# Down's chunks in pairs with seven-product K pairs in a two-layer hybrid decoder trunk

## The chip, the core and the metric

The kernel runs on one core of one Trainium2 chip. The metric is the device time of one execution in microseconds (us). Before the change the median of three runs was 2584.53 us (2582.99 to 2587.38). One execution was profiled; the trace has every instruction of the engines: PE is TensorE (PEld its weight loads), DVE is VectorE, ACT is ScalarE, POOL is GpSimd, and SP is the queue that issues most DMAs.

## The reference

The input is one sequence of 256 tokens with 2048 features in float32. Two layers follow each other: a Mamba-2 state-space mixer and differential attention, each followed by a SwiGLU feed-forward network (FFN). Each of the four sub-layers has an RMSNorm in front and another behind, and the result is added to the residual stream. What matters here is the FFN, which occurs twice:

```
def swiglu(h, w_gate, w_up, w_down):
    return (jax.nn.silu(h @ w_gate) * (h @ w_up)) @ w_down

h = rmsnorm(x, norm_ffn_pre[i])
x = x + rmsnorm(swiglu(h, ffn_w_gate[i], ffn_w_up[i], ffn_w_down[i]), norm_ffn_post[i])
```

Gate and Up are 2048 by 5632 matrices, Down is 5632 by 2048, all in float32.

## The kernel before

**Products.** The 256 tokens make two token tiles of 128 (t = 0, 1). A weight block is read from memory into a `raw` tile (three buffers) and split into a high part `hi` and a remainder `lo` (four buffers each): ScalarE casts `hi` (line 119), VectorE subtracts to get `lo` (line 120). The token side is split in the same way. A float32 product is then three matmuls: high by high, high by low and low by high. Weights are 512 columns wide, so each matmul moves 512 columns past a 128 by 128 token block.

**The plain form, `mv` (line 158).** One chunk of 512 output columns, with K in steps of 128; each step gives both token tiles a product, into one PSUM tile each. A raw tile holds four K steps of one chunk: 24 matmuls.

**The pair form, `pair` (line 201).** Two chunks of 512 columns go together, K in pairs of steps. A raw tile holds two K steps of two chunks, also 24 matmuls. For the K pairs named in `SEVEN` (2, 4 and 6 of eight) the eight products (two token tiles, two K steps, two chunks) are replaced by seven, as in Strassen's and Winograd's scheme for 2 by 2 blocks: 21 matmuls. For that,
- a DMA on POOL's queue adds one weight quarter to another on its way into memory (line 228),
- VectorE makes three sums of weight quarters (lines 242 to 244), and weights and sums are both split: 1536 columns first, then 2048,
- four sums of token blocks, the token *forms*, are split too and used as the token side,
- after the last seven, VectorE combines four PSUM products (lines 259 to 262) into four corrections, which are added or subtracted when an accumulator is evacuated (`done`).

**The FFN.** Chunk 10 is done alone with `mv`; while its Up runs, `make_form` (line 719 on) makes the three token forms and they stay in three of four `xr` buffers. The eleven chunks of 512 hidden features come in three parts: (10, 0, 1), (2, 3, 4, 5) and (6, 7, 8, 9). In each part every two chunks go through a Gate pair and an Up pair; Gate's result stays in a `t512` tile until TensorE transposes the product of Gate and Up (`act_piece`, line 269 on) into the token side for Down. `t512` has eight buffers used in rotation, and a Gate pair with its Up pair takes all eight. Then `out_proj` (line 596 on) runs Down over the part's K steps, for each of its four chunks of 512 output columns with `mv`, and adds up the parts in the eight `m` tiles. In the third part each output chunk is followed by its row sums of squares on ScalarE and by a product with a row of scales on POOL; the row is read by SP into a single `wpost` buffer. Behind the fourth comes the normalisation chain. The residual `x` is kept in memory during the FFN and read back into `xr` buffers for the third part.

**The order of the work.** A planner places the instructions of each engine by its own costs, earlier lines of the program first where they are ready; on the chip each engine then goes through its list in that order. `later(k, ...)` puts a piece of work k ticks later in the program: `pair` and `mv` tick twice for each raw tile. SP issues the raw loads, scale rows and residual; POOL issues the accumulating loads. Each waits at the head of its list until the buffer is free.

Of the kernel before, what the change touches and what calls it, by code (L numbers as in the profile page):

```python
# [10 lines left out]
F32 = mybir.dt.float32  # L11
# [5 lines left out]
P = 128  # L17
S = 256
NT = 2
# [11 lines left out]
LAG2 = 2  # L31

SEVEN = (2, 4, 6)


@with_exitstack
def trunk_kernel(ctx, tc, x_rows, x_cols, vec_cols, vec64, post_rows, lam_rows,
# [110 lines left out]
    def lookup(dct, key):  # L148
        while key not in dct:
            deferred.popleft()[1]()  # L150
        return dct[key]
# [46 lines left out]
                    evac(ct, acc[ct][:, :S], acc[ct][:, S:])  # L198
            tick()

    def pair(blocks, seven, form, done):

        flush()
        acc = {}  # L210
        end = len(blocks) - 1

        def mm(k, st, hi, lo, last):
            first = k not in acc
            if first:
                acc[k] = (auxp.tile([P, 512], F32, tag="aux", name="cp") if isinstance(k, str) else
                          accp.tile([P, 512], F32, tag="acc", name="acc"))
            for q, (a, b) in enumerate(((st[0], hi), (st[0], lo), (st[1], hi))):
                nc.tensor.matmul(acc[k], a, b, start=first and q == 0, stop=last and q == 2)  # L219

        ss = {}
        for kp, src in enumerate(blocks):
            raw = rawp.tile([P, 4, 512], F32, tag="raw", name="raw")
            for c in range(2):
                nc.sync.dma_start(raw[:, 2 * c:2 * c + 2], src[c])
            if kp in seven:

                nc.gpsimd.dma_start(raw[:, 0:1], src[0][:, 1:2], accum_op=ALU.add)
            if kp not in seven:
                hi, lo = prep(raw)  # L230
                for t in range(NT):
                    for c, e in ((0, 2), (1, 0)):
                        for j in range(2):
                            mm((t, c), x_stat(2 * kp + j, t), hi[:, e + j], lo[:, e + j], kp == end and j == 1)
# [7 lines left out]
            nc.vector.tensor_tensor(raw[:, 2], raw[:, 2], raw[:, 0], op=ALU.add)  # L242
            nc.vector.tensor_tensor(raw[:, 3], raw[:, 3], raw[:, 2], op=ALU.add)
            nc.vector.tensor_tensor(raw[:, 1], raw[:, 2], raw[:, 1], op=ALU.subtract)  # L244
            sh, sl = prep(raw)
            k0, k1 = 2 * kp, 2 * kp + 1
            mm("p1", x_stat(k0, 0), hi[:, 1], lo[:, 1], last)
            mm((0, 0), x_stat(k1, 0), hi[:, 2], lo[:, 2], False)
# [5 lines left out]
            mm((1, 0), x_stat(k1, 1), sh[:, 3], sl[:, 3], False)  # L254
            tick()
            if last:
                s1, u, w, x = (t512(n) for n in ("s1", "su", "sw", "sx"))
                nc.scalar.copy(s1, acc["p1"])
                nc.vector.tensor_tensor(u, acc["p6"], s1, op=ALU.subtract)
# [333 lines left out]
        if not final:  # L593
            later(2, stats)

    def out_proj(w, first, last, acts, kgs, step, final, lag, t512, pw, scale=None, ns=range(4)):

        def sums(t, n):
            mt = m[(t, n)]
            row_sumsq(ss4[t][:, n:n + 1], mt, t512("junk"))  # L600
            dst = t512("mw") if n == 3 else mt
            (nc.vector if n == 3 else nc.gpsimd).tensor_tensor(dst, mt, pw(n), op=ALU.mult)
            return dst

        ss4 = {}
        for n in ns:
            def evac(t, ps, n=n):
                if first:
                    m[(t, n)] = mpool.tile([P, 512], F32, tag="m", name="m")
                    nc.scalar.copy(m[(t, n)], ps)  # L610
                else:
                    nc.vector.tensor_tensor(m[(t, n)], m[(t, n)], ps, op=ALU.add)
                if not last:
                    return
                if t not in ss4:
                    ss4[t] = small.tile([P, 4], F32, tag="ss4", name="ss_m", bufs=3)
                    for e in range(n):
                        sums(t, e)
                dst = sums(t, n)
# [7 lines left out]
            def stat(i, j, t):  # L627
                hi, lo = lookup(acts, (t, kgs[i] // 2))
                jj = (kgs[i] % 2) * 2 + j
                return hi[:, jj], lo[:, jj]  # L630
# [52 lines left out]
    def xr_tile(name, shape=(P, 2, 512), dtype=F32):  # L683
        return postp.tile(list(shape), dtype, tag="xr", name=name, bufs=4)

    def fetch_x(src):
# [15 lines left out]
    xr_d = [[dramp.tile([P, 1024], F32, name=f"xr_d{t}{h}") for h in range(2)] for t in range(NT)]  # L702

    def ffn(wg, wu, wd, step, final):
        acts, gt, forms = {}, {}, {}

        def rs(t):
            return lookup(rstd, (step - 1, t))
# [10 lines left out]
        def make_form(kp):  # L719

            n, k = kp // 2, kp % 2 * 2
            xf = t512("xf", (P, NT, 2, P))
            f = t512("f", (P, 4, P))
            for t in range(NT):
                sl = slice(t * P, (t + 1) * P)
                nc.vector.tensor_tensor(xf[:, t], xT_hi[n][:, k:k + 2, sl].bitcast(F32),
                                        xT_lo[n][:, k:k + 2, sl].bitcast(F32), op=ALU.add)
            nc.vector.tensor_tensor(f[:, 0], xf[:, 1, 0], xf[:, 1, 1], op=ALU.subtract)
            nc.vector.tensor_tensor(f[:, 1], xf[:, 1, 0], xf[:, 0, 0], op=ALU.subtract)
            nc.vector.tensor_tensor(f[:, 2], xf[:, 0, 0], f[:, 0], op=ALU.subtract)  # L730
            nc.vector.tensor_tensor(f[:, 3], xf[:, 0, 1], f[:, 2], op=ALU.subtract)
            ff = forms[kp] = xr_tile("ff", (P, 4, 2, P), F32R)
            split(ff[:, :, 0], ff[:, :, 1], f)

        def form(kp, f):
            ff = lookup(forms, kp)
            return ff[:, f, 0], ff[:, f, 1]

        def g_done(p):
            def done(t, c, ps, ss):  # L740
# [25 lines left out]
            for h in range(2):  # L766
                nc.sync.dma_start(xr_d[t][h].rearrange("p (e k) -> p e k", e=2), xr_of[(t, h)])
        for k, kp in enumerate(SEVEN):
            later(1 + 3 * k, lambda kp=kp: make_form(kp))
        mv([wu[10, k] for k in range(4)], u_stat, u_evac, LAG2)  # L770
        parts = [(10, 0, 1), (2, 3, 4, 5), (6, 7, 8, 9)]
        for pi, part in enumerate(parts):
            for c in part:
                if c < 10 and c % 2 == 0:
                    pair(twos(wg, c), SEVEN, form, g_done(c // 2))
                    pair(twos(wu, c), SEVEN, form, u_done(c // 2))
            last = pi == len(parts) - 1
            if last:
                fetch_x(lambda t, h: xr_d[t][h].rearrange("p (e k) -> p e k", e=2))
            out_proj(wd, pi == 0, last, acts, [2 * c + e for c in part for e in range(2)], step, final, LAG2, t512,  # L780
                     load_post(step) if last else None)

    ffn(w_g0, w_u0, w_d0, 1, False)

# [183 lines left out]
```

## Time and profile before

| what | value |
|---|---|
| median of three runs | 2584.53 us |
| the profiled execution | 2586.13 us |
| its span, first to last instruction | 2584.3 us |
| instructions | 31682, of them 12210 matmuls |
| TensorE busy | 2549.0 us (99%) |
| VectorE busy | 1851.3 us (72%) |
| ScalarE busy | 1300.4 us (50%) |
| mean granted TensorE clock | 0.995 |

Matmuls are pipelined: each is recorded with its whole duration, and neighbours overlap, so their spacing (a stretch's length by the matmuls in it) tells more than their length. A row in order of time gives the start, the length, the engine, the line, the operation, the tile written from the tiles read, the shape, and the number of such rows merged; in brackets stands the idle time in front of it and what ended it.

### The profile page before, as it was taken

The numbers are of one execution on the slowest core, as the hardware profiler recorded it, in microseconds if no ns is written. First come the engines' busy times: TensorE is split into PE (matmuls) and PEld (weight loads), VectorE is DVE, ScalarE is ACT, GpSimd is POOL, SyncE is SP. The second block draws the span as 40 slices with busy tenths as digits, with TensorE's granted clock in tenths as the row PEclk, the third lists the DMA queues.
The fourth block names the chain that finished last, engine by engine and source line by source line (L and its number), as shares of the span: only waits on it lengthen the run. The fifth ranks groups of instructions, "written<-read, shape, count | busy, mean of one in ns | idle before, by whom it ended". The sixth has DMA issues, their size and how long they took to land.

```text
span 2584.3 us, 31682 instructions
## 1 busy us (share of the span) xinstructions
PE 2549.0 (99%) x12210; PEld 2096.6 (81%) x12210; DVE 1851.3 (72%) x2280; ACT 1300.4 (50%) x1524; POOL 213.2 (8%) x224
## 2 busy tenths in 40 slices
PE   8999999999999999999999999999999999999998
PEld 7878888888878888888888788887788888888886
DVE  7888757887677668856885665566578478757874
ACT  4555655555565444534453654445555455435542
POOL 2021000111100000000001100000100000000001
PEclk9999999999999999999999999999999999999999
DMA  6545554544766666756676544444566566656663
GB/s 224 186 140 196 182 199 173 196 165 164 266 216 196 218 203 198 228 212 197 196 251 220 190 147 163 179 147 147 211 200 214 202 207 216 232 182 210 211 248 131
DMA packets 120343, 507.87 MB, mean 197 GB/s; under 512 B 11840, under 2 KB 28544, under 8 KB 84352
## 3 DMA queue, kind: packets, MB, share of 16 engines
q1 hardware_dynamic: 110896, 489.27, 53.7%
q0 software_dynamic: 8640, 15.73, 3.7%
q8 instruction: 96, 1.57, 0.3%
q10 hardware_dynamic: 656, 0.85, 0.1%
q14 instruction: 55, 0.45, 0.1%
HBM read 499.44 MB, written 6.36 MB: 196 GB/s over the span
## 4 chain that ended last, share of the span: by engine, by line
PE 94%; DVE 3%; issue 1%; ACT 1%; POOL 0%; DMA 0%; DVEq 0%; POOLq 0%; ACTq 0%
PE acc L168 40%; PE acc L219 26%; PE acc L193 11%; PE cp L219 6%; PE acc L195 6%; PE sc L844 1%; PE pt_f L273 1%; PE py L500 1%; DVE v L425 1%; DVE lo L120 0%; ACT hi L119 0%; PE ptx L576 0%; PE pyt L510 0%; PE po L879 0%; PE pyo L533 0%
## 5 line engine op out<-in xcount | busy, mean ns | idle before, releaser
L120 DVE TENSOR_TENSOR lo<-raw,hi 128x2048 fp32r<-128x2048 f32 (+2 forms) x548 | 1060.7, 1952 | 558.3 <-ACT hi L119 556.8
L119 ACT CAST hi<-raw 128x2048 fp32r<-128x2048 f32 (+2 forms) x548 | 876.8, 1612 | 882.3 <-DVE raw L244 226.3
L219 PE MATMUL acc<-hi,xT 128*128 128x512 f32 x1840 | 589.1, 390 | 0.0
L193 PE MATMUL acc<-xT,hi 128*128 128x512 f32 x1280 | 458.0, 401 | 0.0
L219 PEld LDWEIGHTS acc<-hi,xT 128*128 128x128 f32 x1840 | 345.2, 188 | 71.3
L195 PE MATMUL acc<-xT,lo 128*128 128x256 f32 x1280 | 360.5, 283 | 5.8 <-DVE lo L120 5.8
L219 PE MATMUL acc<-lo,xT 128*128 128x512 f32 x920 | 358.0, 389 | 0.0
L168 PE MATMUL acc<-hi,xT 128*128 128x512 f32 x1024 | 336.3, 400 | 2.3 <-ACT xT L581 1.9
L193 PEld LDWEIGHTS acc<-xT,hi 128*128 128x128 f32 x1280 | 242.0, 189 | 57.7 <-issue 0.9
L168 PE MATMUL acc<-hi,ah_f 128*128 128x512 f32 x704 | 274.5, 391 | 0.0
L168 PE MATMUL acc<-lo,ah_f 128*128 128x512 f32 x704 | 274.4, 390 | 0.0
L168 PE MATMUL acc<-hi,al_f 128*128 128x512 f32 x704 | 274.3, 390 | 0.0
L195 PEld LDWEIGHTS acc<-xT,lo 128*128 128x128 f32 x1280 | 243.5, 190 | 8.2 <-DVE lo L120 6.4
L168 PEld LDWEIGHTS acc<-hi,xT 128*128 128x128 f32 x1024 | 192.8, 189 | 48.6 <-issue 5.1
L168 PE MATMUL acc<-lo,xT 128*128 128x512 f32 x512 | 207.7, 406 | 1.6 <-DVE lo L120 1.6
L219 PEld LDWEIGHTS acc<-lo,xT 128*128 128x128 f32 x920 | 172.7, 188 | 35.7
L168 PEld LDWEIGHTS acc<-hi,al_f 128*128 128x128 f32 x704 | 132.2, 188 | 27.1
L168 PEld LDWEIGHTS acc<-lo,ah_f 128*128 128x128 f32 x704 | 132.2, 188 | 27.0
L168 PEld LDWEIGHTS acc<-hi,ah_f 128*128 128x128 f32 x704 | 132.2, 188 | 26.8
L124 DVE SCALAR_TENSOR_TENSOR lo<-raw,cols,hi 128x512 fp32r<-128x512 f32 x128 | 91.6, 762 | 52.1 <-ACT hi L123 51.8
L219 PE MATMUL cp<-hi,ff 128*128 128x512 f32 x360 | 120.7, 389 | 0.0
L168 PEld LDWEIGHTS acc<-lo,xT 128*128 128x128 f32 x512 | 97.0, 189 | 24.1 <-issue 3.9
(248 smaller groups left out, 2843.3 us busy)
## 6 DMA issues: line engine op xcount, KB each, us to landing
raw<-in_w_d_dram SPq DMA_DIRECT2D x88, 1024.0 KB, 4.8
raw<-in_w_zxbc_dram SPq DMA_DIRECT2D x80, 1024.0 KB, 4.8
raw<-in_w_g_dram SPq DMA_DIRECT2D x160, 512.0 KB, 4.5
raw<-in_w_u_dram SPq DMA_DIRECT2D x160, 512.0 KB, 4.9
raw<-in_w_qkv_dram SPq DMA_DIRECT2D x48, 1024.0 KB, 4.7
raw<-in_w_so_dram SPq DMA_DIRECT2D x32, 1024.0 KB, 4.8
raw<-in_w_ao_dram SPq DMA_DIRECT2D x16, 1024.0 KB, 4.8
mt<-acum_d SPq DMA_DIRECT2D x16, 512.0 KB, 6.7
```

Of the source, the lines that this page charges most:

```text
L119: nc.scalar.copy(hi, raw)
L120: nc.vector.tensor_tensor(lo, raw, hi.bitcast(F32), op=ALU.subtract)
L124: nc.vector.scalar_tensor_tensor(lo[:, j], raw[:, j], scale[j], hi[:, j].bitcast(F32), op0=ALU.mult, op1=ALU.subtract)
L168: nc.tensor.matmul(acc[t], a, b[:, j], start=(i == 0 and j == 0 and q == 0), stop=(i == last and j == 1 and q == 2))
L193: nc.tensor.matmul(acc[ct], hi[:, j, cs], x.rearrange("p a s -> p (a s)"), start=(i == 0 and j == 0), stop=False)
L195: nc.tensor.matmul(acc[ct][:, :S], lo[:, j, cs], x[:, 0], start=False, stop=(i == last and j == 1))
L219: nc.tensor.matmul(acc[k], a, b, start=first and q == 0, stop=last and q == 2)
L273: nc.tensor.transpose(pt[:, j], src[:, j * P:(j + 1) * P], ident)
L425: nc.vector.scalar_tensor_tensor(v, u[:, k:k + S], cwh[:, ch, k:k + 1], v, op0=ALU.mult, op1=ALU.add)
L500: nc.tensor.matmul(py[e * 64:(e + 1) * 64, a], xd[c][:, 2 * a + e], mts[c][:, 2 * a + e], start=True, stop=True)
L844: nc.tensor.matmul(sc[c][:, h], qT[cp, h, ts], kT[cp, h, :nk * P], start=True, stop=True)
```

## The change

`out_proj` gets two new arguments. `two` lists output chunks that are done in pairs with `pair`, before `mid` (a function called once) and before the chunks in `ns`, which still use `mv`. In parts one and two Down's four output chunks are two pairs, (0, 1) and (2, 3). In part three they are one pair, (0, 1), then the residual is read back, then chunks 2 and 3 go with `mv`.

In each Down pair two K pairs take seven products: numbers 2 and 4 where the part has six K pairs (part one), 2 and 5 where it has eight. Their token forms are made from the split activations by `make_form` with four additions of 128 columns in place of two of 256 and then the same steps. They are queued with `later(max(0, 2 * i - 4), ...)` from the start of the part's first Down pair and used by both pairs of the part. In part one the K pairs are put in the order 20, 0, 21, 1, 2, 3, so that the first form comes from chunk 10.

Evacuation adds the correction to the PSUM tile as in Gate and Up, into a new `m` tile in part one, and with a second addition to `m` in the other parts.

The Gate and Up forms no longer stay in their buffers through the FFN. They are written to memory once made (`keep`, on SP) and read back by POOL's queue at the start of parts two and three, so that the four `xr` buffers serve both kinds of forms in rotation.

In part three the row sums and scale products of chunks 0 and 1 are queued two ticks behind the pair; those of chunks 2 and 3 stay behind their chunks.

```
+DSEVEN = {6: (2, 4), 8: (2, 5)}
...
-    def pair(blocks, seven, form, done):
+    def pair(blocks, stat, seven, form, done):
...
-    def out_proj(w, first, last, acts, kgs, step, final, lag, t512, pw, scale=None, ns=range(4)):
+    def out_proj(w, first, last, acts, kgs, step, final, lag, t512, pw, scale=None, ns=range(4), two=(), mid=None):
...
+        def row(t, e):
+            if t not in ss4:
+                ss4[t] = small.tile([P, 4], F32, tag="ss4", name="ss_m", bufs=3)
+            if e not in summed[t]:
+                summed[t].add(e)
+                return sums(t, e)
+
         ss4 = {}
+        summed = {t: set() for t in range(NT)}
+        forms = {}
+        seven = DSEVEN[len(kgs)] if two else ()
+        for n in two:
+            def done(t, c, ps, ss, n=n):
+                y, op = ss[(t, c)]
+                k = (t, n + 1 - c)
+                if first:
+                    m[k] = mpool.tile([P, 512], F32, tag="m", name="m")
+                    nc.vector.tensor_tensor(m[k], ps, y, op=op)
+                else:
+                    nc.vector.tensor_tensor(y, ps, y, op=op)
+                    nc.vector.tensor_tensor(m[k], m[k], y, op=ALU.add)
+
+            if n == two[0]:
+                for i in seven:
+                    later(max(0, 2 * i - 4), lambda i=i: make_form(forms, i, stat, t512))
+            pair([[w[n + e, kg // 2][:, kg % 2 * 2:kg % 2 * 2 + 2] for e in range(2)] for kg in kgs],
+                 stat, seven, lambda i, f: form_of(lookup(forms, i), f), done)
+            if last:
+                later(2, lambda n=n: [row(t, e) for e in (n, n + 1) for t in range(NT)])
+        if mid:
+            mid()
...
+    def make_form(dct, key, stat, t512, keep=None):
+
+        xf = t512("xf", (P, NT, 2, P))
+        f = t512("f", (P, 4, P))
+        for t in range(NT):
+            for j in range(2):
+                hi, lo = stat(key, j, t)
+                nc.vector.tensor_tensor(xf[:, t, j], hi.bitcast(F32), lo.bitcast(F32), op=ALU.add)
...
+        ff = dct[key] = xr_tile("ff", (P, 4, 2, P), F32R)
+        split(ff[:, :, 0], ff[:, :, 1], f)
+        if keep:
+            nc.sync.dma_start(keep, ff.rearrange("p f h q -> p (f h q)").bitcast(F32))
...
         for pi, part in enumerate(parts):
+            if pi:
+                for kp in SEVEN:
+                    forms[kp] = xr_tile("ff", (P, 4, 2, P), F32R)
+                    nc.gpsimd.dma_start(forms[kp].rearrange("p f h q -> p (f h q)"), keep[kp])
...
+            kgs = [2 * c + e for c in part for e in range(2)]
+            if pi == 0:
+                kgs[1:3] = kgs[2], kgs[1]
+            if pi < len(parts) - 1:
+                out_proj(wd, pi == 0, False, acts, kgs, step, final, LAG2, t512, None, ns=(), two=(0, 2))
+            else:
+                out_proj(wd, False, True, acts, kgs, step, final, LAG2, t512, load_post(step), ns=range(2, 4),
+                         two=(0,), mid=lambda: fetch_x(lambda t, h: xr_d[t][h].rearrange("p (e k) -> p e k", e=2)))
```

More of the change, by code (lines that the diff above doesn't have):

```diff
@@ L233, in pair @@
                         for j in range(2):
-                            mm((t, c), x_stat(2 * kp + j, t), hi[:, e + j], lo[:, e + j], kp == end and j == 1)
+                            mm((t, c), stat(kp, j, t), hi[:, e + j], lo[:, e + j], kp == end and j == 1)
                         if kp == end:
@@ L245, in pair @@
             sh, sl = prep(raw)
-            k0, k1 = 2 * kp, 2 * kp + 1
-            mm("p1", x_stat(k0, 0), hi[:, 1], lo[:, 1], last)
-            mm((0, 0), x_stat(k1, 0), hi[:, 2], lo[:, 2], False)
+            mm("p1", stat(kp, 0, 0), hi[:, 1], lo[:, 1], last)
+            mm((0, 0), stat(kp, 1, 0), hi[:, 2], lo[:, 2], False)
             mm((0, 1), form(kp, 3), hi[:, 0], lo[:, 0], False)
@@ L253, in pair @@
             mm("p7", form(kp, 1), sh[:, 0], sl[:, 0], last)
-            mm((1, 0), x_stat(k1, 1), sh[:, 3], sl[:, 3], False)
+            mm((1, 0), stat(kp, 1, 1), sh[:, 3], sl[:, 3], False)
             tick()
@@ L603, in sums, with stat @@
             return dst
-        ss4 = {}
+        def stat(i, j, t):
+            hi, lo = lookup(acts, (t, kgs[i] // 2))
+            jj = (kgs[i] % 2) * 2 + j
+            return hi[:, jj], lo[:, jj]
+        def row(t, e):
[4 more added lines that the diff above has]
+                return sums(t, e)
+        ss4 = {}
+        summed = {t: set() for t in range(NT)}
[20 more added lines that the diff above has]
+            mid()
         for n in ns:
@@ L614, in evac @@
                     return
[L615 to L619, printed above, removed]
+                for e in range(n):
+                    row(t, e)
+                dst = row(t, n)
                 if n == 2:
@@ L684, in xr_tile, with form_of @@
         return postp.tile(list(shape), dtype, tag="xr", name=name, bufs=4)
+    def make_form(dct, key, stat, t512, keep=None):
[5 more added lines that the diff above has]
+                nc.vector.tensor_tensor(xf[:, t, j], hi.bitcast(F32), lo.bitcast(F32), op=ALU.add)
+        nc.vector.tensor_tensor(f[:, 0], xf[:, 1, 0], xf[:, 1, 1], op=ALU.subtract)
+        nc.vector.tensor_tensor(f[:, 1], xf[:, 1, 0], xf[:, 0, 0], op=ALU.subtract)
+        nc.vector.tensor_tensor(f[:, 2], xf[:, 0, 0], f[:, 0], op=ALU.subtract)
+        nc.vector.tensor_tensor(f[:, 3], xf[:, 0, 1], f[:, 2], op=ALU.subtract)
+        ff = dct[key] = xr_tile("ff", (P, 4, 2, P), F32R)
+        split(ff[:, :, 0], ff[:, :, 1], f)
+        if keep:
+            nc.sync.dma_start(keep, ff.rearrange("p f h q -> p (f h q)").bitcast(F32))
+    def form_of(ff, f):
+        return ff[:, f, 0], ff[:, f, 1]
     def fetch_x(src):
@@ L704, in ffn @@
     def ffn(wg, wu, wd, step, final):
-        acts, gt, forms = {}, {}, {}
+        acts, gt, forms, keep = {}, {}, {}, {}
         def rs(t):
@@ L717, in u_evac, with kp_stat @@
             acts[(t, 10)] = act_piece(g, f"f{step}_10_{t}")
[L719 to L733, printed above, removed]
+        def kp_stat(kp, j, t):
+            return x_stat(2 * kp + j, t)
         def form(kp, f):
-            ff = lookup(forms, kp)
-            return ff[:, f, 0], ff[:, f, 1]
+            return form_of(lookup(forms, kp), f)
         def g_done(p):
@@ L768, in ffn @@
         for k, kp in enumerate(SEVEN):
-            later(1 + 3 * k, lambda kp=kp: make_form(kp))
+            keep[kp] = dramp.tile([P, 8 * P], F32, name=f"form{step}_{kp}")
+            later(1 + 3 * k, lambda kp=kp: make_form(forms, kp, kp_stat, t512, keep[kp]))
         mv([wu[10, k] for k in range(4)], u_stat, u_evac, LAG2)
@@ L772, in ffn @@
         for pi, part in enumerate(parts):
+            if pi:
+                for kp in SEVEN:
+                    forms[kp] = xr_tile("ff", (P, 4, 2, P), F32R)
+                    nc.gpsimd.dma_start(forms[kp].rearrange("p f h q -> p (f h q)"), keep[kp])
             for c in part:
                 if c < 10 and c % 2 == 0:
[L775 to L781, printed above, removed]
+                    pair(twos(wg, c), kp_stat, SEVEN, form, g_done(c // 2))
+                    pair(twos(wu, c), kp_stat, SEVEN, form, u_done(c // 2))
+            kgs = [2 * c + e for c in part for e in range(2)]
[6 more added lines that the diff above has]
+                         two=(0,), mid=lambda: fetch_x(lambda t, h: xr_d[t][h].rearrange("p (e k) -> p e k", e=2)))
     ffn(w_g0, w_u0, w_d0, 1, False)
```

4 lines of the change are left out of this document (removed).

## The prediction

> **What bounds the kernel now.** I read the page first, then a view of busy time by stretches, then VectorE and TensorE in order of time around the chunk boundaries of the FFN. The page's busy times:
>
> ```profile
> PE 2549.0 (99%) x12210; PEld 2096.6 (81%) x12210; DVE 1851.3 (72%) x2280; ACT 1300.4 (50%) x1524; POOL 213.2 (8%) x224
> PE 94%; DVE 3%; issue 1%; ACT 1%; POOL 0%; DMA 0%; DVEq 0%; POOLq 0%; ACTq 0%
> ```
>
> TensorE is busy nearly all the time and holds 94% of the chain that ended last, so a matmul that goes away can be worth its place. Its worth is not its mean duration of 390 ns, because neighbours overlap. The stretch view (columns: length, then busy time and count for PE, PEld, DVE, ACT, POOL; then clock, DMA share, GB/s) gives the spacing:
>
> ```profile
> 930.00:970.00 40.00, 40.00 (x178) 33.14 (x177) 30.09 (x25) 21.38 (x15) 1.75 (x2) 1.00 0.63 200
> 1100.00:1140.00 40.00, 40.00 (x178) 33.09 (x177) 22.48 (x14) 13.62 (x8) 0.00 (x0) 1.00 0.63 226
> 996.50:1025.10 28.60, 28.60 (x136) 23.68 (x135) 25.13 (x26) 15.13 (x13) 1.75 (x2) 1.00 0.53 171
> ```
>
> The first stretch is a gate pair with seven-product K pairs, the second is Down as it is now. Both hold 178 matmuls in 40 us: 0.225 us each, with no hole. But VectorE is busy for 75% of the gate pair against 56% of Down, and in the third stretch, the passage from an Up pair to the next Gate pair, for 88%. Its rows there, in order of time (start, length, instruction; in brackets idle time and its cause):
>
> ```profile
> 997.57 6.88 DVE L120 TENSOR_TENSOR lo<-raw,hi 128x2048 fp32r<-128x2048 f32 x3 [2.11 <-ACT hi L119]
> 1004.36 0.68 DVE L259 TENSOR_TENSOR su<-cp,s 128x512 f32<-128x512 f32 x1
> ...
> 1011.63 0.75 DVE L753 SCALAR_TENSOR_TENSOR sx<-sx,rs_pre 128x512 f32<-128x512 f32 x1
> 1012.29 1.28 DVE L267 TENSOR_TENSOR al_f<-pt_f,ah_f 128x512 fp32r<-128x512 f32 x2
> 1013.49 2.28 DVE L120 TENSOR_TENSOR lo<-raw,hi 128x2048 fp32r<-128x2048 f32 x1
> 1015.69 1.28 DVE L267 TENSOR_TENSOR al_f<-pt_f,ah_f 128x512 fp32r<-128x512 f32 x2
> 1016.89 1.75 DVE L120 TENSOR_TENSOR lo<-raw,hi 128x1536 fp32r<-128x1536 f32 x1
> 1018.67 0.69 DVE L242 TENSOR_TENSOR raw<-raw 128x512 f32<-128x512 f32 x1
> 1019.40 0.69 DVE L243 TENSOR_TENSOR raw<-raw 128x512 f32<-128x512 f32 x1
> 1020.01 0.68 DVE L244 TENSOR_TENSOR raw<-raw 128x512 f32<-128x512 f32 x1
> 1022.71 6.16 DVE L120 TENSOR_TENSOR lo<-raw,hi 128x2048 fp32r<-128x2048 f32 x3 [2.02 <-ACT hi L119]
> ```
>
> From 997.57 to 1020.7 there is no idle row: three splits, the combinations of the Up pair, its evacuation and products, four activation pieces, the split of K pair 1, and the first half of K pair 2, which is a seven. Then come 2.02 us in which ScalarE must cast the sums, and the split of the sums, 2.28 us, ends at 1025.0. TensorE's rows for the product that needs it:
>
> ```profile
> 1024.87 0.39 PE L219 MATMUL cp<-hi,ff 128*128 128x512 f32 x1
> 1025.09 0.47 PE L219 MATMUL cp<-lo,ff 128*128 128x512 f32 x1
> 1025.40 0.62 PE L219 MATMUL cp<-hi,ff 128*128 128x512 f32 x2
> ```
>
> The second of them reads that split at 1025.09 and its successor comes 0.31 instead of 0.23 us later. So VectorE's margin at this passage is 0.1 us: TensorE is the bound on average, VectorE here. Down after an Up pair has this margin to spare today only because its blocks are plain: one 2.29 us split for 5.43 us of matmuls (24 by 0.226).
>
> **The change part by part.** *Removed:* a seven-product K pair takes 21 matmuls where the plain one takes 24. Each FFN gets two sevens in each of two Down pairs in parts one and two, and in one pair in part three: 10, in both FFNs 20. That is 60 matmuls by 0.226 us, -13.6 us, all on the bounding engine.
>
> *Added, splits and combinations:* per seven, VectorE splits 1536 and 2048 columns and makes three sums (1.75 + 2.07 + 2.28 us by the rows above, 6.1 in place of 2.3); per pair, four combinations and four or eight evacuating adds at 0.6 us. In a Down pair of eight K pairs that is 6 by 2.2 + 2 by 6.1 + 2.8 + 5, about 33 us against 42 us of matmuls. The second Down pair of a part, and the Gate pair behind it, keep their cover; I cost them nothing. Without this cover a second pair would pay what the first pays below.
>
> *Added, the token forms, two per part:* what one costs VectorE is seen where Gate's forms are made today:
>
> ```profile
> 749.66 0.75 DVE L726 TENSOR_TENSOR xf<-xT 128x256 f32<-128x256 f32 x2
> 750.45 0.29 DVE L728 TENSOR_TENSOR f<-xf 128x128 f32<-128x128 f32 x1
> 750.66 0.28 DVE L729 TENSOR_TENSOR f<-xf 128x128 f32<-128x128 f32 x1
> 750.86 0.28 DVE L730 TENSOR_TENSOR f<-xf,f 128x128 f32<-128x128 f32 x1
> 751.17 0.29 DVE L731 TENSOR_TENSOR f<-xf,f 128x128 f32<-128x128 f32 x1
> 753.79 0.68 DVE L267 TENSOR_TENSOR ff<-f,ff 128x512 fp32r<-128x512 f32 x1
> ```
>
> 749.66 to 751.46 is 1.8 us, and four xf adds of half the width instead of two make it 1.85; with the split, 2.5 us a form. Where does it stand? The first form is queued behind the first half of Down's K pair 0, ahead of the splits of K pairs 1 and 2. It cannot go up into the Up pair: its xf and f take the two oldest of eight t512 buffers, and those hold the Gate pair's products until TensorE transposes them, 1010.33 and 1013.94 in the chain's pieces here:
>
> ```profile
> 1010.33 0.87 PE pt_f L273 x8
> 1011.20 2.74 PE acc L219 x12
> 1013.94 0.87 PE pt_f L273 x8
> ```
>
> So its 2.5 us fall into the dense stretch, and K pair 2's sums are late by 2.5 less 0.1. The bounds: 0.5 us if all of it fell into the 2.02 us gap behind the sums, 2.5 if none does. I take 2.5, since it is queued ahead of what surrounds the gap and its inputs are long there. In part one the second form (K pair 4) is queued ahead of K pair 2 as well and costs another 2.5, bounds 0.5 and 2.5. In parts two and three (K pair 5) it is queued behind K pair 2: its adds fill the gap, and two plain blocks give 2 by 3.1 us behind; I take 0, or 0.6 if its split stands alone.
>
> Parts two and three also enter with less. In their last Up pair the last sums' split begins at 1083.53 for products at 1087.26, 3.7 us ahead; in the pair quoted above at 997.57 for 1002.16, 4.6 us ahead:
>
> ```profile
> 1083.53 6.70 DVE L120 TENSOR_TENSOR lo<-raw,hi 128x2048 fp32r<-128x2048 f32 x3 [2.11 <-ACT hi L119]
> ...
> 1087.26 2.04 PE cp L219 x9
> ...
> 1002.16 2.04 PE cp L219 x9
> ```
>
> That is 0.9 us. TensorE then waits 2.5 + 2.5 - 0.1 = 4.9 us in part one, 2.5 + 0.9 - 0.1 = 3.3 in each of the others: 11.5 per FFN, 23.0 in all.
>
> *Moved and queued elsewhere:* three form stores of 512 KB on SP, six reloads on POOL's queue per FFN, two more accumulating loads per pair. The stores stand near the Up loads of chunk ten, where raw blocks run far ahead. A reload waits until TensorE has left its buffer, and accumulating loads stand behind it; today's issues are 8 to 20 us apart and land in 3.8:
>
> ```profile
> raw<-in_w_u_dram POOLq DMA_DIRECT2D x30, 256.0 KB, 3.8
> x<-xr_d SPq DMA_DIRECT2D x8, 512.0 KB, 6.1
> wpost<-in_post_rows_dram SPq DMA_DIRECT2D x18, 256.0 KB, 4.8
> ```
>
> I cost them 0, at most one landing of 3.8 us in each of the four later parts, 15 us. The row sums move into the time of the third Down chunk: two more scale-row loads wait there for POOL products and hold SP's raw loads behind them. I cost 0; the cover is the 21.7 us of matmuls of a chunk (96 by 0.226), and the price without it is again a landing, 4.8 us per FFN.
>
> *Sum:* -13.6 + 23.0 = +9.4. The profiled execution took 2586.13 us (span 2584.3 and 1.8 around it), which would become 2595.5; the median of the runs, 2584.53, is 1.6 lower, so 2594.
>
> One rule speaks for more. After TensorE has waited, the clock view shows this at the start of the first FFN:
>
> ```profile
> 727.44:730.85 3.41, 1.62 (x6) 0.76 (x5) 2.86 (x8) 3.41 (x7) 0.00 (x0) 1.00 0.37 99
> 730.85:734.26 3.41, 3.40 (x8) 2.73 (x9) 3.41 (x11) 2.48 (x9) 1.52 (x2) 0.50 0.64 265
> ```
>
> A stretch with TensorE busy for 1.62 of 3.41 us is followed by one at half clock, which loses 1.7 us. The Trainium skill, "TensorE: Matmul & The Clock Gate", Part 1, says that the clock falls to half after an idle window of about 3.4 us; by that rule stalls of two pieces below 3.4 us would cost nothing beyond themselves, though this trace halves after less.
>
> **The rivals.** *The forms are hidden (faster).* Place: VectorE ahead of K pair 2 in each part's first Down pair. If the order puts every form into the gaps behind the sums, each form costs 0.5: 0.9 us in part one, 1.3 in each other, 7 in all, and 13.6 - 7 gives 2578; with more margin than the trace shows, up to 2571. It decides below 1 us per form. For it: the gap of 2.02 us before each second split stands empty today. Against it: the form's work is ready before the gap and queued first.
>
> *Half and half.* Part one's second form hidden, the entry margin as large as in the earlier pairs: 2.4 us in each of six places, 14 us: 2585, no change.
>
> *The clock drops too.* If each of six stalls is followed by a half-clock stretch outside the wait, 6 by 1.7 adds 10 us: 2604. Against it: the slow stretch may lie inside the time in which VectorE is behind anyway.
>
> *Queues.* The reload ahead of an accumulating load, as priced above: 2594 + 15 at worst; little speaks for it, since a buffer is left one pair or more before its form is needed again.
>
> **How the numbers follow.** Forecast 0.40, around 2590 to 2598; clock or queues on top, 0.11, up to 2604 and beyond; half and half 0.18; forms hidden 0.31. Within 0.2% (5.2 us, what a measurement of this kernel can tell from no change) lies the third. So slower 0.51, same 0.18, faster 0.31. The range leaves out the ends: 2574 to 2601; the forecast's own is 2590 to 2598.
>
> **What would show it.** TensorE should have 12150 matmuls. Right: waits on VectorE's splits at K pairs 1 and 2 of each first Down pair, about 2 to 5 us, none in second pairs; L726-like adds standing ahead of K pair 1 or 2. Wrong: TensorE unbroken through the first Down pair with form adds in the gap behind the sums; or waits at another place, for a DMA or at a pair's end.

## The result, and the profile after

| what | before | after |
|---|---|---|
| median of four runs each, same chip | 2584.12 us | 2603.86 us (2602.93 to 2607.45) |
| profiled execution, its span | 2586.13, 2584.3 us | 2604.7, 2602.9 us |
| mean granted TensorE clock | 0.995 | 0.993 |

The ratio is 1.0074, with a 95% interval of 1.0061 to 1.0088: the change makes the kernel slower by 19.7 us, 0.7%. The forecast had the direction, 2594 us, but its range ended at 2601.

The page of the kernel after, busy times and chain by engine:

```profile
PE 2546.5 (98%) x12150; PEld 2086.4 (80%) x12150; DVE 2000.1 (77%) x2560; ACT 1329.8 (51%) x1550; POOL 242.8 (9%) x256
PE 78%; DVE 10%; DMA 4%; issue 4%; ACT 3%; POOL 0%; SPq 0%; DVEq 0%; ACTq 0%; POOLq 0%
```

The 60 matmuls are gone, 13.6 us at their spacing, yet TensorE's busy time falls by only 2.5 us: a matmul is recorded longer where it does not follow another closely (0.50 us against 0.39 in rows below), and a stretch at half clock, shown further down, has longer ones too. VectorE works 149 us more. The chain has moved: TensorE held 94% of it and now holds 78%; VectorE has 10% instead of 3%, and a DMA, which had none, 4%. The view of waits, TensorE's, cut to the lines of the pair (what waited, for whom; in total, times, longest):

```profile
PE cp L221 <- DVE lo L122: 11.9, 9, 1.8
...
PE cp L221 <- ACT hi L121: 3.8, 4, 1.3
...
PE acc L221 <- DVE lo L122: 2.1, 4, 0.7
...
PE acc L221 <- ACT hi L121: 1.7, 4, 0.6
...
PE acc L221 <- DVE sw L633: 1.5, 2, 0.8
```

Before, none of these rows existed for the pair's line: its matmuls (line 219 there) had no wait in the first dozen rows of that view. These are 21 us; the longer matmuls around each wait add to it. For the full price I took every K pair of Down from TensorE's records: the time from its first matmul to the next K pair's first, less 21 or 24 by 0.2266 us (the spacing where TensorE runs through). What is left over, in us ("first" and "second" are a part's Down pairs; K pairs not listed are at 0.1 or below; K pair 0's extra, which is its transposes, is left out):

| Down pair | K pair 1 | K pair 2 (seven) | later seven | forecast, K pairs 1 to 4 |
|---|---|---|---|---|
| FFN 1, part one, first | 0 | 2.49 | 0.56 (K pair 4) | 4.9 |
| FFN 1, part two, first | 1.00 | 1.49 | **2.94** (K pair 5) | 3.3 |
| FFN 1, part two, second | 0 | 0 | **0.31** | 0 |
| FFN 1, part three, first | 0.78 | 1.53 | **4.50** | 3.3 |
| FFN 2, part one, first | 0 | 2.49 | 0.56 (K pair 4) | 4.9 |
| FFN 2, part two, first | 0.77 | 1.54 | **2.01** | 3.3 |
| FFN 2, part two, second | 0 | 0 | **1.47** | 0 |
| FFN 2, part three, first | 0.83 | 1.52 | **1.38** | 3.3 |

With what K pair 3 has (0.1 us or less each), K pairs 1 to 4 cost 16.0 us where 23.0 was forecast. K pair 5 costs 12.6 us where nothing was. The third item is the evacuation row above (L633), about 2 us at the Gate pair behind part two. Together 30.6 us; less 13.6 us that is +17.0. The remaining 1.6 us of the 18.6 us lie almost wholly ahead of the FFN: the first Gate pair starts at 778.0 us instead of 776.7, in code that the change doesn't touch.

Two stalls follow in detail, both in part two's first Down pair of the first FFN. VectorE in order of time (start, length, instruction; in brackets the idle time before it and its cause):

```profile
1101.31 0.90 DVE L725 TENSOR_TENSOR xf<-ah_f,al_f 128x128 f32<-128x128 f32 x4
1102.11 1.29 DVE L268 TENSOR_TENSOR al_f<-pt_f,ah_f 128x512 fp32r<-128x512 f32 x2
1103.31 0.29 DVE L726 TENSOR_TENSOR f<-xf 128x128 f32<-128x128 f32 x1
1103.51 0.29 DVE L727 TENSOR_TENSOR f<-xf 128x128 f32<-128x128 f32 x1
1103.71 0.29 DVE L728 TENSOR_TENSOR f<-xf,f 128x128 f32<-128x128 f32 x1
1103.91 2.29 DVE L122 TENSOR_TENSOR lo<-raw,hi 128x2048 fp32r<-128x2048 f32 x1
1106.11 0.29 DVE L729 TENSOR_TENSOR f<-xf,f 128x128 f32<-128x128 f32 x1
1106.32 1.76 DVE L122 TENSOR_TENSOR lo<-raw,hi 128x1536 fp32r<-128x1536 f32 x1
1107.98 0.69 DVE L268 TENSOR_TENSOR ff<-f,ff 128x512 fp32r<-128x512 f32 x1
...
1112.71 2.29 DVE L122 TENSOR_TENSOR lo<-raw,hi 128x2048 fp32r<-128x2048 f32 x1 [0.36 <-ACT hi L121]
...
1121.22 1.76 DVE L122 TENSOR_TENSOR lo<-raw,hi 128x1536 fp32r<-128x1536 f32 x1 [1.21 <-ACT hi L121]
1126.54 0.69 DVE L244 TENSOR_TENSOR raw<-raw 128x512 f32<-128x512 f32 x1 [3.56 <-DMA raw<-in_w_d_dram]
```

The first stall is the one forecast. The form's additions (lines 725 to 729) stand ahead of K pair 1's split at 1103.91, the last one right behind it; the form's own split (line 268 with `ff`) stands between the two splits of K pair 2. TensorE answers (same columns, only its rows with idle time):

```profile
1106.26 0.50 PE L221 MATMUL acc<-lo,ah_f 128*128 128x512 f32 x1 [0.66 <-DVE lo L122]
...
1115.06 0.50 PE L221 MATMUL cp<-lo,ff 128*128 128x512 f32 x1 [1.14 <-DVE lo L122]
...
1130.69 0.50 PE L221 MATMUL cp<-hi,ff 128*128 128x512 f32 x1 [0.53 <-ACT hi L121]
1133.02 0.50 PE L221 MATMUL cp<-lo,ff 128*128 128x512 f32 x1 [1.82 <-DVE lo L122]
```

The second stall, at 1130.69 and 1133.02, is new. TensorE waits for ScalarE and VectorE, but they are late themselves: at 1126.54 VectorE's first sum of K pair 5 had waited 3.56 us for a DMA. POOL's queue and two stretches (length, then busy time and count of PE, PEld, DVE, ACT, POOL, clock, DMA share, GB/s) show which:

```profile
1118.76 0.89 POOL L230 DMA_DIRECT2D raw<-in_w_d_dram  x1 [19.97 <-DMA raw<-in_w_d_dram]
```

```profile
1106.00:1118.70 12.70, 11.30 (x48) 8.74 (x49) 12.27 (x19) 6.66 (x5) 0.00 (x0) 1.00 0.44 160
1118.70:1126.50 7.80, 7.80 (x36) 6.48 (x35) 3.07 (x2) 1.49 (x1) 0.89 (x1) 1.00 0.98 287
```

The accumulating load is issued at 1118.76, after a wait for the plain load of the same tile, and VectorE can go on at 1126.5: 7.7 us. While it is under way the DMA engines are 98% busy with the next raw loads; in the 12.7 us before they were at 44%. The raw tiles rotate over three buffers, so K pair 5 has the buffer of K pair 2, and that one, a seven, is held until its sums have been split (to 1115.0, the row at 1112.71): nothing could be loaded into it earlier. The DMA view has the medians by kind (KB each, median us from issue to landing):

```profile
raw<-in_w_u_dram POOLq DMA_DIRECT2D x30, 256.0 KB, 3.8
ff<-form POOLq DMA_DIRECT2D x12, 512.0 KB, 6.8
raw<-in_w_d_dram POOLq DMA_DIRECT2D x20, 256.0 KB, 5.5
```

The prediction took 3.8 us for an accumulating load from Gate and Up. Down's take 5.5.

### The profile page after: what moved, and what is told of

Same layout as the page of the kernel before. It is cut to its first block, busy times and chain, and to the rows that moved or that the text cites. A ratio compares the mean times of both kernels' runs of the same rounds, so it can differ in the third digit from the quotient of the medians.

```text
span 2602.9 us, 32242 instructions
## 1 busy us (share of the span) xinstructions
PE 2546.5 (98%) x12150; PEld 2086.4 (80%) x12150; DVE 2000.1 (77%) x2560; ACT 1329.8 (51%) x1550; POOL 242.8 (9%) x256
## 4 chain that ended last, share of the span: by engine, by line
PE 78%; DVE 10%; DMA 4%; issue 4%; ACT 3%; POOL 0%; SPq 0%; DVEq 0%; ACTq 0%; POOLq 0%
PE acc L221 26%; PE acc L170 24%; PE acc L195 11%; PE cp L221 6%; PE acc L197 6%; DMA raw<-in_w_d_dram 4%; DVE lo L122 3%; ACT hi L121 3%; PE sc L891 1%; PE py L501 1%; DVE v L426 1%; DVE raw L244 1%; DVE raw L245 1%; DVE al_f L268 0%; DVE raw L246 0%
## 5 line engine op out<-in xcount | busy, mean ns | idle before, releaser
L122 DVE TENSOR_TENSOR lo<-raw,hi 128x2048 fp32r<-128x2048 f32 (+2 forms) x568 | 1094.6, 1948 | 417.4 <-ACT hi L121 415.8
L121 ACT CAST hi<-raw 128x2048 fp32r<-128x2048 f32 (+2 forms) x568 | 903.1, 1607 | 869.1 <-DVE raw L246 344.5
L221 PE MATMUL acc<-hi,xT 128*128 128x512 f32 x1840 | 589.8, 390 | 1.5 <-DVE sw L633 1.5
L221 PEld LDWEIGHTS acc<-hi,xT 128*128 128x128 f32 x1840 | 345.3, 188 | 73.6 <-DVE sw L633 2.3
L221 PE MATMUL acc<-lo,xT 128*128 128x512 f32 x920 | 358.0, 389 | 0.0
L221 PEld LDWEIGHTS acc<-lo,xT 128*128 128x128 f32 x920 | 172.8, 188 | 35.7
L221 PE MATMUL acc<-lo,ah_f 128*128 128x512 f32 x456 | 178.5, 391 | 2.1 <-DVE lo L122 2.1
L221 PE MATMUL acc<-hi,al_f 128*128 128x512 f32 x456 | 178.0, 390 | 0.0
L221 PE MATMUL acc<-hi,ah_f 128*128 128x512 f32 x456 | 174.5, 393 | 1.7 <-ACT hi L121 1.7
L221 PE MATMUL cp<-hi,ff 128*128 128x512 f32 x480 | 162.9, 393 | 3.8 <-ACT hi L121 3.8
L125 ACT ACTIVATE hi<-raw,cols 128x512 fp32r<-128x512 f32 x128 | 84.5, 715 | 55.7 <-PE acc L170 39.1
L221 PEld LDWEIGHTS cp<-hi,ff 128*128 128x128 f32 x480 | 90.0, 189 | 24.3 <-ACT hi L121 6.5
L221 PE MATMUL cp<-lo,ff 128*128 128x512 f32 x240 | 96.4, 402 | 11.9 <-DVE lo L122 11.9
```

The lines of the kernel that those rows point to most:

```text
L121: nc.scalar.copy(hi, raw)
L122: nc.vector.tensor_tensor(lo, raw, hi.bitcast(F32), op=ALU.subtract)
L125: nc.scalar.activation(hi[:, j], raw[:, j], AF.Copy, scale=scale[j])
```

## The experiments

All are edits of the kernel after, unless said otherwise; "before" was timed beside them (2584.98, 2585.05, 2585.74 and 2584.4 us in the four groups).

For each, the table gives what TensorE lost in both FFNs. It is worked out from the records: the time from the start of the first product of the first Gate pair to the start of the last product of the last Down pair, in both FFNs, less the same time without any seven (second row, 1241.6 us), plus 0.2266 us for each matmul removed.

| kernel | matmuls less | both stretches, us | lost in waits, us | ratio to before [95%] |
|---|---|---|---|---|
| after | 60 | 1258.6 | 30.6 | 1.0074 [1.0061, 1.0088] |
| no seven | 0 | 1241.6 | 0 | 1.0001 [0.9991, 1.001] |
| no reloads | 60 | 1257.0 | 29.0 | 1.0075 [1.006, 1.009] |
| no forms | 60 | 1250.8 | 22.8 | 1.004 [1.0025, 1.0055] |
| sevens 2 and 6 | 60 | 1263.3 | 35.3 | 1.0108 [1.0093, 1.0123] |
| VectorE adds | 60 | 1256.5 | 28.5 | 1.0051 [1.0034, 1.0068] |
| forms later | 60 | 1255.9 | 27.9 | 1.0061 [1.0045, 1.0078] |
| sevens 3 and 5 | 48 | 1235.2 | 4.5 | 0.9981 [0.9972, 0.9991] |
| sevens 3 and 5, VectorE adds | 48 | 1245.8 | 15.1 | 1.0005 [0.9995, 1.0014] |
| seven 4 alone | 30 | 1235.2 | 0.4 | 0.9977 [0.9966, 0.9987] |
| sevens 3 and 5, forms later | 48 | 1232.1 | 1.4 | 0.9959 [0.9946, 0.9971] |

### Does anything but the sevens cost?

```
-DSEVEN = {6: (2, 4), 8: (2, 5)}
+DSEVEN = {6: (), 8: ()}
```

(and `done` evacuates without a correction)

> Edit: Down's chunks go in pairs as in the change, with stores and reloads of the forms and the row sums behind the pair, but no K pair takes seven products, so Down has no forms, sums, accumulating loads or corrections. Theory: pairing and rotation cost nothing by themselves, 2583 to 2587 us, as before the change. Rival: a part of the loss comes from pairing, reloads or row sums, 2588 us or more.

Measured: 2585.77 us (2582.27 to 2587.8), the time of before. The pairing of the chunks, the stores and reloads, the moved row sums and the residual behind the pair cost nothing. The whole loss belongs to the sevens in Down and their forms.

### The reloads

```
-                    nc.gpsimd.dma_start(forms[kp].rearrange("p f h q -> p (f h q)"), keep[kp])
+                    nc.gpsimd.memset(forms[kp].rearrange("p f h q -> p (f h q)").bitcast(F32), 0.0)
```

Gate and Up of parts two and three then compute with zeros for forms.

> Edit: the Gate and Up forms are not read back in parts two and three; POOL fills the buffers with zeros (the products with them are then wrong in value, not in number). Theory (buffer): the six reloads per FFN cost little, 2600 to 2604 us. Rival (crowded DMA engines): without them the accumulating loads land in time and 8 us or more come back, 2596 us or less.

Measured: 2604.2 us (2602.77 to 2605.96). K pair 5's waits in the first pairs are 2.62, 1.59, 1.54 and 1.81 us (10.8 us after), but part one of the second FFN waits 4.06 us instead of 2.49, and the time doesn't move. Both differences go in the main with one half-clock stretch (the next run shows what that is): the kernel after has it behind K pair 5, in the 4.50 us, and this one behind the 4.06 us, where TensorE is busy for 1.51 us of 2014.30 to 2017.71 and the next 3.41 us run at clock 0.50. The six reloads per FFN aren't the cause.

### The forms taken away

```
+        if not keep:
+            dct[key] = [stat(key, j, t) for t in range(NT) for j in range(2)]
+            return
```

(`form_of` returns these; Down's sevens multiply by the split activations themselves, without a token sum)

> Edit: Down's token forms are not computed; the sevens use the split activations themselves as the token side (as many matmuls, other values). Theory of the prediction: the forms' work on VectorE stands ahead of K pair 2 and makes the waits at K pairs 1, 2 and 4 of the first Down pairs, 16.0 us in all; without it 0 us in part one and up to 0.8 us in each other part remain, the waits at K pair 5 stay: about 2590 us. Rival: those waits come from the denser pair itself (splits, sums, casts), then 2600 us or more.

Measured: 2594.81 us (2591.38 to 2599.92). K pairs 1 to 4 of all first pairs now cost 1.6 us instead of 16.0: the forms are the cause of the first stall. But 14 us less there moved the time by only 9. K pair 5 costs more, 4.53, 6.16, 3.94 and 4.50 us. Stretches of part two's first Down pair here show why:

```profile
1124.20:1127.60 3.40, 1.08 (x4) 0.34 (x2) 2.27 (x2) 3.40 (x4) 0.00 (x0) 1.00 0.00 0
1127.60:1131.02 3.42, 3.35 (x8) 2.67 (x9) 3.42 (x4) 1.77 (x1) 0.00 (x0) 0.51 0.73 254
```

TensorE works 1.08 of 3.40 us, and the next stretch runs at half clock: 8 matmuls in 3.42 us instead of 15, some 1.6 us lost. There are five such stretches behind K pair 5 in this kernel, one in the kernel after:

```profile
1390.97:1394.38 3.41, 1.07 (x4) 0.55 (x4) 2.60 (x2) 3.41 (x4) 0.00 (x0) 1.00 0.00 0
1394.38:1397.80 3.42, 3.42 (x9) 2.65 (x9) 3.42 (x3) 1.45 (x1) 0.00 (x0) 0.50 0.77 266
```

So four more half-clock stretches, 6 to 7 us, took back about what K pair 5 grew by (19.1 against 12.6 us). By the Trainium skill, "TensorE: Matmul & The Clock Gate", Part 1, the clock falls after an idle window of about 3.4 us. Here a window with a third of it busy is enough, and in the prediction's rows one nearly half busy was. A busier one was not: the window that lies 152 such lengths (3.413 us) ahead of 1394.38 in the kernel after, in part one's first stall, has TensorE busy for 1.99 us, and full clock follows.

```profile
875.56:878.97 3.41, 1.99 (x8) 1.00 (x6) 2.00 (x3) 3.29 (x2) 0.00 (x0) 1.00 0.97 278
878.97:882.38 3.41, 2.94 (x13) 2.39 (x14) 3.41 (x3) 1.80 (x2) 0.00 (x0) 1.00 0.51 150
```

### The second seven at another place

```
-DSEVEN = {6: (2, 4), 8: (2, 5)}
+DSEVEN = {6: (2, 4), 8: (2, 6)}
```

> Edit: in the parts with eight K pairs the second seven is K pair 6 instead of 5; nothing else. Theory: K pair 5 goes into the raw buffer of K pair 2 (three buffers, three blocks later), which a seven keeps until its sums are split, so its loads and the accumulating load behind them start late; K pair 6 goes into the buffer of K pair 3, which is free early. Then the waits at the second seven (10.8 us in first Down pairs, 1.8 us in second ones, summed over both FFNs) go, and the waits at K pairs 1 and 2 (16.0 us) stay: about 2591 us. Rival, the DMA engines are crowded by the added loads themselves: the waits move with the seven, 2600 to 2604 us.

Measured: 2612.41 us (2610.32 to 2615.67), a miss by some 20 us. In part two the wait of the late seven is gone in all four pairs (0.03 us or less at K pair 6), as expected of a buffer that comes from a plain K pair. In part three it is there, 2.96 and 4.33 us. The residual is read back beside it there (SP issues two reads of 512 KB from 1383.61 on); that these reads are the reason is likely, but no run leaves them out. The accumulating load issued at 1385.18 is waited for until 1394.13, 8.9 us, while the DMA engines carry 343 GB/s. A stretch, POOL's row and VectorE's row of that kernel:

```profile
1380.00:1390.00 10.00, 10.00 (x46) 8.32 (x45) 6.78 (x4) 3.40 (x2) 0.87 (x1) 1.00 1.02 343
```

```profile
1385.18 0.87 POOL L230 DMA_DIRECT2D raw<-in_w_d_dram  x1 [25.93 <-DMA raw<-in_w_d_dram]
```

```profile
1394.13 0.69 DVE L244 TENSOR_TENSOR raw<-raw 128x512 f32<-128x512 f32 x1 [5.16 <-DMA raw<-in_w_d_dram]
```

A new wait came besides: with the last seven near the pair's end, the corrections run late, and VectorE's list has a split of the next pair's weights among them. From the second Down pair to Gate:

```profile
1185.33 2.29 DVE L122 TENSOR_TENSOR lo<-raw,hi 128x2048 fp32r<-128x2048 f32 x1 [3.37 <-ACT hi L121]
1187.54 0.68 DVE L261 TENSOR_TENSOR sw<-cp,su 128x512 f32<-128x512 f32 x1
1188.14 0.68 DVE L633 TENSOR_TENSOR s<-acc,s 128x512 f32<-128x512 f32 x1
```

VectorE stands 3.37 us in front of a Gate block that has landed late (ScalarE's cast of it, at 1183.38, had waited 4.67 us for `raw<-in_w_g_dram`), with the corrections behind it, and TensorE cannot reuse the accumulators: the row `PE acc L221 <- DVE s L633` has 5.4 us there. Three half-clock stretches in this kernel's pairs (6.83 us from 1188.12 and 3.41 from 2543.21) are part of its 35.3 us. A seven can thus be too late in a pair as well as too early.

### The accumulating load replaced by VectorE

```
-            if kp in seven:
+            if kp in seven and not vadd:
                 nc.gpsimd.dma_start(raw[:, 0:1], src[0][:, 1:2], accum_op=ALU.add)
...
+            if vadd:
+                nc.vector.tensor_tensor(raw[:, 0], raw[:, 0], raw[:, 1], op=ALU.add)
```

(`vadd` only in Down's pairs)

> Edit: in Down's sevens VectorE adds the two weight quarters (128x512, 0.7 us) and no accumulating load is issued; all else as in the change. Theory: at K pair 5 VectorE waits for the accumulating load, which lands 7 to 8 us after its issue; without it the sums can start some 3.5 us earlier in each of the four first pairs, so most of the 10.8 us of waits there and of the 1.8 us in second pairs goes; at the first seven, where VectorE is the bound, each of six pairs loses 0.6 us, in part one two times: about 2604 - 11 + 5 = 2598 us. Rival, the raw loads themselves are late by as much as the accumulating load: the waits at K pair 5 stay above 2 us each, 2604 to 2609 us.

Measured: 2598.41 us (2597.25 to 2599.4). The expected number came out by luck. K pair 5's wait is 0.00 us in all six places where it had 12.6: the accumulating load is its cause. But most of what it gains is lost in front of K pair 2, which has one VectorE addition more ahead of it: 5.91 and 5.06 us in part one, 2.35 to 3.89 in the others, with five half-clock stretches behind these waits. K pairs 1 to 4 cost 28.5 us instead of 16.0, where 5 more had been expected, and the waits of both FFNs together fall by 2.1 us only. Much of the rest lies elsewhere: the spans of the two profiled executions differ by 7.5 us, and 4.2 of them (778.03 less 773.86) lie ahead of all that was changed: the first Gate pair starts earlier by that much.

### Sevens at K pairs 3 and 5, with either way of adding

```
-DSEVEN = {6: (2, 4), 8: (2, 5)}
+DSEVEN = {6: (3,), 8: (3, 5)}
```

> Edit: Down's sevens are K pairs 3 and 5 of eight and K pair 3 of six (48 matmuls fewer than before the change, 10.9 us, in place of 60). Theory: VectorE gets one plain block more (3.1 us) ahead of the first seven, which covers the 2.2 to 2.5 us of a form, and K pair 5 now uses the raw buffer of a plain K pair, so little of either wait is left: 2574 to 2580 us, faster than before the change. Rival, the waits follow the sevens because loads and VectorE are too busy anywhere in a pair: 2585 us or more.

Measured: 2580.22 us (2578.37 to 2582.98), faster than before. The first seven comes 5.4 us of TensorE's work later and K pair 5 no longer has the buffer of the seven before it. What is left are 0.8 us at K pair 1 and 0.3 us at K pair 5 in four places.

The same, and VectorE adds in place of the accumulating load:

> Edit: both, sevens at 3 and 5 of eight and at 3 of six, and VectorE's addition in place of the accumulating load. Theory: if the run with the sevens at 3 and 5 has waits for accumulating loads left, this has not, and VectorE has the 0.7 us to spare there: 2574 to 2578 us. Rival: VectorE has nothing to spare, slower than the run with the accumulating loads.

Measured: 2586.5 us (2582.42 to 2591.94), 6.3 us above the kernel it was compared with. VectorE has no time to give in the first Down pairs even here; K pair 1 waits 0.8 to 2.0 us where it waited 0.8, and K pair 3 has 1.0 us where it had none.

### One seven in the middle

```
-DSEVEN = {6: (2, 4), 8: (2, 5)}
+DSEVEN = {6: (4,), 8: (4,)}
```

> Edit: one seven per Down pair, K pair 4, with one form per part (30 matmuls fewer than before the change, 6.8 us). Theory: two plain blocks more ahead of it, no second seven: no waits, 2578 us, 2576 to 2581. Rival: each form's 2.2 us on VectorE shows as a wait wherever it stands, six of them 13 us, 2590 us.

Measured: 2578.42 us (2576.96 to 2582.59). From K pair 1 on no K pair of Down waits at all, and 30 matmuls bring what they weigh: 30 by 0.2266 is 6.8 us, measured 6.6.

### The forms a block later

```
-                    later(max(0, 2 * i - 4), lambda i=i: make_form(forms, i, stat, t512))
+                    later(2 * i - 2, lambda i=i: make_form(forms, i, stat, t512))
```

with the sevens of the change:

> The kernel of the change with its own sevens (K pairs 2 and 4 of six, 2 and 5 of eight); only the form's place moves, one block later on VectorE's list (two half-blocks ahead of its use in place of four). If the form's place ahead of K pair 1's and K pair 2's splits is what the first seven waits for (16 us in the changed kernel), most of these waits go, K pair 5's 12.6 us with the accumulating load behind them stay, and the time is 2590 to 2594 us. The rival: VectorE enters the first Down pair with no margin, and wherever the form stands ahead of K pair 2's products it delays them: then the wait only moves to K pair 2 and the time stays within 3 us of 2604 us.

Measured: 2599.86 us (2597.95 to 2602.33), 4.0 us better than the change in another group, with intervals that overlap, and between the two expectations. K pairs 1 to 4 cost 11.9 instead of 16.0 us, K pair 5 12.5 (two half-clock stretches among them). So most of the first stall stays when the form moves by one block with its seven still at K pair 2. With sevens at K pairs 3 and 5 there is room:

> Sevens at K pairs 3 and 5 of eight and 3 of six, each form queued one block later than in the kernel of the change (two half-blocks ahead of its use in place of four). 48 matmuls are gone as in the run with sevens 3 and 5, -10.9 us. There TensorE waited 0.8 us at K pair 1 of the first Down pair of parts two and three, four places, 3.2 us, because the first form stood ahead of K pair 1's split. If that is the cause, these waits go, K pair 5's 0.3 us stay, and the time is about 2577 us. The rival: VectorE is short of time over the whole pair, then the form only moves the wait to K pair 3, 0.8 us or more in each of the same four places, and the time stays at 2580 us.

Measured: 2576.2 us (2572.91 to 2576.83). The 0.8 us at K pair 1 are gone in all four places. VectorE's rows show the order that does it: two blocks are split before the form's work is finished.

```profile
1097.27 2.29 DVE L122 TENSOR_TENSOR lo<-raw,hi 128x2048 fp32r<-128x2048 f32 x1
1099.47 1.29 DVE L268 TENSOR_TENSOR al_f<-pt_f,ah_f 128x512 fp32r<-128x512 f32 x2
1100.67 0.90 DVE L725 TENSOR_TENSOR xf<-ah_f,al_f 128x128 f32<-128x128 f32 x4
1101.47 0.29 DVE L727 TENSOR_TENSOR f<-xf 128x128 f32<-128x128 f32 x1
1101.68 0.29 DVE L726 TENSOR_TENSOR f<-xf 128x128 f32<-128x128 f32 x1
1101.88 2.29 DVE L122 TENSOR_TENSOR lo<-raw,hi 128x2048 fp32r<-128x2048 f32 x1
```

Beside it the single seven was run again:

> The kernel with one seven at K pair 4 of each Down pair, beside the one with its forms queued later, on the same chip: 30 matmuls less, no wait of TensorE, 2578 us as before. If the late forms are worth their place, the two are within 2 us of each other, and the pair of sevens is ahead by 1 to 2; if VectorE is short of time, the single seven is ahead by 2.

Measured: 2579.17 us (2577.43 to 2582.78; ratio 0.9977, 0.9966 to 0.9987). Two sevens with late forms are 3.0 us ahead of it, though the intervals overlap at their ends (0.9971 and 0.9966); the slowest of its five runs, 2576.83 us, is below the fastest of the other's eight, 2577.43. This version beats before by 0.4%, and the change by 27.7 us by medians of different groups; it keeps all else of the change.

## Why the prediction was right and wrong

**Right: what is removed.** 60 matmuls at 0.2266 us. Where nothing waits, they bring their full weight (seven 4 alone).

**Right in place, too large in size: the forms on VectorE.** The step said that each form's 2.5 us stand ahead of K pair 2 in the first Down pairs and go to TensorE whole: 4.9 and 3.3 us per pair, 23.0 in all. The waits are where it put them, and without forms they fall from 16.0 to 1.6 us. The term measured 16.0. A form takes 2.2 us, since four independent additions of 128 columns, and likewise the dependent ones interleaved with splits, come 0.2 us apart; the second form's split in part one ran in the gap before the sums' split, which kept 1.41 of its 2.02 us:

```profile
875.51 0.69 DVE L268 TENSOR_TENSOR ff<-f,ff 128x512 fp32r<-128x512 f32 x1
877.61 6.16 DVE L122 TENSOR_TENSOR lo<-raw,hi 128x2048 fp32r<-128x2048 f32 x3 [1.41 <-ACT hi L121]
```

By these sizes part one would lose 2.2 + 2.2 - 0.6 - 0.1 = 3.7 us and the others 3.0; measured are 3.1 and 2.4 to 2.6. The last half microsecond per pair is not accounted for.

**Wrong: "I cost them 0", the accumulating loads.** This is the step that failed. It took 3.8 us from Gate's and Up's loads, with 8 to 20 us between issues, and its bound, one landing in each later part, was set to zero. Measured are 12.6 us at K pair 5, in all four later parts and in the second pairs too. The bound of 15 us held in the sum alone: it allowed one landing of 3.8 us in each later part, and one part lost 4.50. Two things were missed. Gate and Up have their sevens two apart on three raw buffers, so no seven follows another in its buffer; Down's 2 and 5 are three apart and share one. The rival looked at the form's reload ahead of the load on POOL's queue, which the run without reloads shows to be harmless, instead of at what the load itself waits for. And a load that starts late runs beside the raw loads that were held up with it: 7.7 us instead of 3.8. By the Trainium skill, "DMA: Bandwidth & Descriptors", on the anatomy of one DMA on the GpSimd path, 256 KB would take an estimated 2.6 us; the trace has more in either case.

**Wrong: "I cost them nothing", the second pairs' cover.** K pair 5 costs 1.8 us there, the evacuation behind them about 2. It is the same load: it makes the last seven's combinations late, and with VectorE's additions in its place both waits are gone.

**Right: the other parts costed at nothing.** Pairing, splits in second pairs, stores, reloads, row sums: the kernel without sevens runs in the time of before.

**Partly right: the clock.** The rival had six half-clock stretches, 10 us. The kernel after has one in the FFN's pairs. They become the price in the variants with longer waits: five without forms, five with VectorE's additions, three with sevens 2 and 6.

Of the forecast's +9.4 us, then, the form term was 7 us too high, while K pair 5 with the evacuation behind it, 14.6 us, had no term. The clock rival's 2604 us meets the measured time by luck: one stretch in place of its six, and another cause. The rival on the queues had the right kind of loss, a late accumulating load, with the wrong reason for it, and "little speaks for it" was the misjudgement.

## What to carry to other kernels

Before a step with several stages is put into a loop over rotating buffers, count which step used the same buffer last and when that one lets go: two long holders that fall on one buffer start each other's loads late. Price a small DMA by the load on the engines at the moment when it will run, not by its median elsewhere. When the engine that prepares the data has no margin at the entry of a stage, its extra work belongs later in the stage: here half as many sevens, or sevens that begin one block further in with their forms queued a block later, beat the full set.

## What the runs showed of the hardware

- An accumulating load of 256 KB takes 3.8 us (median) among Gate's and Up's loads, 7.7 us with the DMA engines 98% busy, and 8.9 us at 343 GB/s.
- The granted clock halves for 3.4 us after a window in which TensorE was busy for 1.07 of 3.41 us, though its longest gap was 1.59 us, and does not after one with 1.99. With such a stretch behind it, K pair 5's wait cost 4.5 us, where 1.4 to 2.9 us were lost in the other first pairs.
